# Folding the gate sums to 64 partitions before their product with ones

## The chip, the cores and the metric

The kernel runs on one NeuronCore of a Trainium2 chip. The metric is the device time of one execution in microseconds (us), the lower the better. Three timed executions of the kernel before took 1096.84, 1097.05 and 1098.40 us; the median is 1097.05 us. One more execution was recorded by the profiler, and all traces below are from it.

The engines are named as the profile does it: PE is the matrix engine (PEld its loading of stationary operands), DVE the vector engine, ACT the scalar engine, POOL the general engine (gpsimd), SP the one that issues the weight DMAs. Each engine works through its own list of instructions in order and waits at an instruction until what it needs is there.

## The reference, cut to what matters

```python
def reference(x, c, ada_w, ada_b, ...):              # x: 256 tokens x 1024, two layers
    c_act = jax.nn.silu(c)                            # c: 1 x 1024
    for l in range(DEPTH):
        mod = c_act @ ada_w[l] + ada_b[l]
        sh1, sc1, g1, sh2, sc2, g2, sh3, sc3, g3 = jnp.split(mod, N_ADA, axis=-1)
        n1 = modulate(rms_norm(h, norm_g[l, 0]), sh1, sc1)
        h = h + 0.5 * g1[:, None, :] * swiglu(n1, ...)
        n2 = modulate(rms_norm(h, norm_g[l, 1]), sh2, sc2)
        h = h + g2[:, None, :] * token_mixing(n2, ...)
        n3 = modulate(rms_norm(h, norm_g[l, 2]), sh3, sc3)
        h = h + 0.5 * g3[:, None, :] * swiglu(n3, ...)
    return rms_norm(h, final_g)
```

The change touches only how the gates g1, g2 and g3 (1024 numbers for each of the six sub-layers) are brought to all 128 partitions.

## The kernel before, in words

The two layers have three sub-layers each: a feed-forward network (FFN), the token mixer, and a second FFN. They run one after the other, with all 256 tokens at once. In the FFN, the 2816 hidden columns are cut into 11 slices (`idx` 0 to 10, `NS = 11`): for each slice a gate bank `g` and an up bank `u` are computed (`gate_up_mm`, then `gate_up_act`), and some slices later the down product `dn` (`down`). The mixer ends with eight gate products (`gate_mm`, tile `gt`), the output heads (`b_out`, `b_outT`, tiles `on`, `onf`, `odH`, `odL`), and then the branch products `yb` (`merge`) and `wo`.

All products are made in a split form: an operand in 32-bit floating point is taken as a high part (a rounded copy, made by ACT: `whi`, `hh`, `gh`) and a low part (what is left, made by DVE: `wlo`, `hl`, `gl`), and `mm3` (lines 85 to 88) forms a product as high·high, low·high and high·low. The weights come in by DMA into the ring `raw` (4 buffers), and `pump` splits them ahead of their use.

The gates are made in two steps. First `ada_gate` (line 276) multiplies a block of the weights with one element of silu(c) per partition and adds it to `gacc` (128 partitions x 1024 columns), eight times for each sub-layer; row 0 of `gacc` begins with the bias. What is then missing is the sum over the 128 partitions, and that sum on every partition. `gate_bcast` (lines 289 to 304) gives both by a product with a 128x128 matrix of ones: for each half of 512 columns, ACT makes `gh` (line 299), DVE makes `gl` (line 300), PE adds the products of ones with `gh` and with `gl` in one bank `gb` (lines 301, 302), and ACT writes half of the sum to `g` (tile `gbc`, line 304). `residual` uses it much later, at the end of the sub-layer.

`gate_bcast` is called once for each sub-layer: after slice 7 of each FFN (or when the weights of the next gate are about to be loaded, line 282), and in the mixer between the last gate product and the first `yb`. This document calls the six places A to F: A, FFN 1 of layer 0 (at 139.8 us of the trace); B, its mixer (323.2 us); C, its second FFN (451.3 us); D, FFN 1 of layer 1 (624.8 us); E, the second mixer (858.5 us); F, the last FFN (1028.5 us).

The order of instructions on each engine is not the order of the program text: a scheduler lays the instructions out at build time by its own costs and by what they depend on. POOL's list is short: it clears `gacc` (line 286), and raises small tiles to the power -1/2 (`pow_half`, line 124). `b2` tiles (tags `gh`, `gl`, `sg`, `on` and others) come from one ring of 8 buffers.

Of the kernel before, what the change touches and what calls it, by code (L numbers as in the profile page):

```python
# [13 lines left out]
F32 = mybir.dt.float32  # L14
F32R = mybir.dt.float32r
AF = mybir.ActivationFunctionType
ALU = mybir.AluOpType
AX = mybir.AxisListType

P = 128  # L20
# [22 lines left out]
def trunk(tc, a):  # L43
    nc = tc.nc
    with (
# [11 lines left out]
        def nm(s):  # L57
            uid[0] += 1
            return f"{s}_{uid[0]}"

        def gen(name="gen"):
            return ps.tile([P, 512], F32, tag="gen", bufs=4, name=nm(name))
# [4 lines left out]
        def b2(name, shape=(P, 512), dt=F32):  # L67
            return sb.tile(list(shape), dt, tag="b2", bufs=NB2, name=nm(name))
# [13 lines left out]
        def const(name, shape, dt=F32):  # L82
            return sb.tile(list(shape), dt, tag=name, bufs=1, name=name)
# [29 lines left out]
        onesr = const("onesr", [P, P], F32R)  # L113
        nc.scalar.copy(onesr, ones)
        for hf in range(2):
            x = slice(hf * 512, (hf + 1) * 512)
            bank = gen("cb")
# [162 lines left out]
        def gate_start(l, s):  # L280
            if owed:
                gate_bcast(*owed[0])
            owed.append((l, s))
            m = mod_of(l, s)
            m["gacc"] = sb.tile([P, D], F32, tag="gacc", bufs=1, name=nm("gacc"))
            nc.gpsimd.memset(m["gacc"], 0.0)
            nc.scalar.dma_start(m["gacc"][0:1, :], a["ada_b_row"][l, s:s + 1, :])

        def gate_bcast(l, s):
            m = mods[(l, s)]  # L290
            if (l, s) not in owed:
                return
            owed.remove((l, s))
            m["g"] = sb.tile([P, D], F32, tag="gbc", bufs=1, name=nm("gbc"))
            for hf in range(2):
                bank = gen("gb")
                x = m["gacc"][:, hf * 512:(hf + 1) * 512]
                gh, gl = b2("gh", dt=F32R), b2("gl", dt=F32R)
                nc.scalar.copy(gh, x)
                nc.vector.tensor_tensor(gl, x, gh.bitcast(F32), op=ALU.subtract)  # L300
                nc.tensor.matmul(bank, onesr, gh, start=True, stop=False, skip_group_check=True)
                nc.tensor.matmul(bank, onesr, gl, start=False, stop=True, skip_group_check=True)

                nc.scalar.mul(m["g"][:, hf * 512:(hf + 1) * 512], bank, 0.5)

# [255 lines left out]
        def ffn(i, nT, norm1, first, nT_next):  # L561
# [64 lines left out]
            for idx in range(start, NS):  # L626
                g, u = gen("g"), gen("u")
                gate_up_mm(g, u, unit(idx), nT)
                hT[idx] = gate_up_act(g, u)
                if idx == 7:  # L630
                    gate_bcast(l, s)
                if idx == 1:
                    hT[0] = first_T(hts)
                elif idx - 1 < NS - TAIL:
                    if idx == 2 and first is None:
                        down(0)
                    down(idx - 1)
                if idx == 4 and s == 0:
                    consts = mixer_loads(l)
                if idx == 7 and s == 0:  # L640
                    consts = mixer_consts(l, consts)
# [75 lines left out]
        def mixer(i, nT, norm1, consts, nT_next):  # L717
# [373 lines left out]
            b_outT(1)  # L1091
            gate_mm(7, 1)
            gate_bcast(l, 1)


# [310 lines left out]
```

## Time and profile before

| | |
|---|---|
| median of three runs | 1097.05 us (1096.84 to 1098.40) |
| the profiled execution | 1097.68 us |
| its span, first to last instruction | 1095.9 us |
| PE busy | 99% of the span, 7796 recorded products |
| DVE, ACT, POOL busy | 79%, 54%, 4% |
| granted PE clock, mean | 0.999 of full speed |

The profiled execution takes 1.8 us more than its span, which is start and end around the instructions. Products on PE overlap: one of 512 columns has a recorded duration of 0.39 us, but the next one begins 0.23 us after it. So what a product costs is read from the distance of two starts, not from its duration. On ACT and DVE too, an instruction begins about 0.1 us before the one ahead of it has ended, when nothing else holds it.

### The profile page before, as it was taken

How to read it: one execution, taken by the hardware profiler on the slowest of the kernel's cores; microseconds unless marked ns; L12 is line 12 of the kernel's file. 1: busy time of each engine (PE TensorE's matmuls, PEld its weight loads, DVE VectorE, ACT ScalarE, POOL GpSimd, SP SyncE). 2: the span in 40 equal slices, each digit the busy share in tenths (PEclk: the TensorE clock that was granted, in tenths of full speed). 3: DMA queues.
4: the chain of work that ended last, by engine and by line, in shares of the span. 5: the costliest groups of instructions: out<-in, count | busy, mean ns of one | idle time of the engine just before them, and what ended most of it. 6: DMA issues, size and time to landing. Idle time of an engine off the chain costs nothing.

```text
span 1095.9 us, 19235 instructions
## 1 busy us (share of the span) xinstructions
PE 1082.9 (99%) x7796; PEld 998.8 (91%) x7796; DVE 864.9 (79%) x1388; ACT 593.1 (54%) x916; POOL 44.5 (4%) x52
## 2 busy tenths in 40 slices
PE   8999999999999999999999999999999999999997
PEld 6989999898999899999989999989889998999996
DVE  5998986899978798886589886569988779766543
ACT  5564483558664554535455545435776547444432
POOL 1000000220010000000000000004000000000000
PEclk9999999999999999999999999999999999999999
DMA  8998996368745299997449987543865454876501
GB/s 315 380 368 336 380 335 219 120 263 332 264 172 193 86 376 357 347 377 266 150 152 357 365 288 285 202 165 126 297 236 189 157 190 183 315 267 229 197 19 39
DMA packets 44889, 271.12 MB, mean 247 GB/s; under 512 B 5880, under 2 KB 6648, under 8 KB 14848
## 3 DMA queue, kind: packets, MB, share of 16 engines
q1 hardware_dynamic: 42340, 267.93, 66.1%
q10 hardware_dynamic: 2460, 1.96, 0.6%
q8 instruction: 61, 1.00, 0.3%
q14 instruction: 28, 0.23, 0.1%
HBM read 268.82 MB, written 1.05 MB: 246 GB/s over the span
## 4 chain that ended last, share of the span: by engine, by line
PE 94%; DVE 3%; ACT 1%; issue 1%; POOL 0%; POOLq 0%
PE dn L87 6%; PE dn L88 6%; PE dn L86 6%; PE u L86 6%; PE g L86 6%; PE u L87 6%; PE g L88 6%; PE g L87 6%; PE u L88 6%; PE gt L86 3%; PE gt L88 3%; PE gt L87 3%; PE g L1199 2%; PE u L1199 2%; PE yb L88 1%; PE yb L87 1%
## 5 line engine op out<-in xcount | busy, mean ns | idle before, releaser
L330 DVE TENSOR_TENSOR wlo<-raw,whi 128x1024 fp32r<-128x1024 f32 x364 | 436.9, 1220 | 133.7 <-PE u L87 44.6
L328 ACT CAST whi<-raw 128x1024 fp32r<-128x1024 f32 x364 | 374.0, 1052 | 226.4 <-PE u L88 83.7
L86 PE MATMUL u<-nh,whi 128*128 128x256 f32 x592 | 164.0, 277 | 0.0
L86 PE MATMUL g<-nh,whi 128*128 128x256 f32 x592 | 164.0, 277 | 0.0
L87 PE MATMUL u<-nh,wlo 128*128 128x256 f32 x592 | 163.7, 277 | 0.0
L88 PE MATMUL g<-nl,whi 128*128 128x256 f32 x592 | 163.7, 277 | 0.0
L87 PE MATMUL g<-nh,wlo 128*128 128x256 f32 x592 | 163.7, 277 | 0.0
L88 PE MATMUL u<-nl,whi 128*128 128x256 f32 x592 | 163.6, 276 | 0.0
L86 PE MATMUL dn<-whi,hh 128*128 128x512 f32 (+1 forms) x326 | 126.0, 387 | 0.0
L87 PE MATMUL dn<-whi,hl 128*128 128x512 f32 (+1 forms) x326 | 125.9, 386 | 0.0
L88 PE MATMUL dn<-wlo,hh 128*128 128x512 f32 (+1 forms) x326 | 125.8, 386 | 0.0
L86 PEld LDWEIGHTS g<-nh,whi 128*128 128x128 f32 x592 | 111.2, 188 | 0.3
L87 PEld LDWEIGHTS g<-nh,wlo 128*128 128x128 f32 x592 | 111.2, 188 | 0.2
L86 PEld LDWEIGHTS u<-nh,whi 128*128 128x128 f32 x592 | 111.2, 188 | 0.1
L87 PEld LDWEIGHTS u<-nh,wlo 128*128 128x128 f32 x592 | 111.3, 188 | 0.0
L88 PEld LDWEIGHTS u<-nl,whi 128*128 128x128 f32 x592 | 111.2, 188 | 0.2
L88 PEld LDWEIGHTS g<-nl,whi 128*128 128x128 f32 x592 | 111.2, 188 | 0.0
L245 DVE CUSTOM_DVE_ANT_0 raw<-raw,cb 128x1024 f32<-128x1024 f32 x80 | 95.5, 1217 | 1.1 <-DMA raw<-in_ada_t_dram 0.9
L86 PE MATMUL gt<-nh,whi 128*128 128x256 f32 x256 | 73.7, 288 | 0.0
L88 PEld LDWEIGHTS dn<-wlo,hh 128*128 128x128 f32 x326 | 61.2, 188 | 12.4
L87 PEld LDWEIGHTS dn<-whi,hl 128*128 128x128 f32 x326 | 61.3, 188 | 11.1 <-DVE hl L546 0.2
L86 PEld LDWEIGHTS dn<-whi,hh 128*128 128x128 f32 x326 | 61.3, 188 | 11.1
(227 smaller groups left out, 2051.9 us busy)
## 6 DMA issues: line engine op xcount, KB each, us to landing
raw<-in_w_gu_dram SPq DMA_DIRECT2D x79, 1024.0 KB, 5.5
raw<-in_w_d_dram SPq DMA_DIRECT2D x41, 1024.0 KB, 6.4
raw<-in_ada_t_dram SPq DMA_DIRECT2D x40, 1024.0 KB, 6.8
raw<-in_ada_g_dram SPq DMA_DIRECT2D x24, 1024.0 KB, 6.3
raw<-in_w_in_dram SPq DMA_DIRECT2D x16, 1024.0 KB, 5.0
raw<-in_w_gate_dram SPq DMA_DIRECT2D x16, 1024.0 KB, 4.9
raw<-in_ada_t_dram SPq DMA_DIRECT2D x16, 512.0 KB, 6.5
raw<-in_w_gu_dram SPq DMA_DIRECT2D x32, 256.0 KB, 6.1
```

The lines of the kernel that those rows point to most:

```text
L86: nc.tensor.matmul(out, Lh, Rh, start=start, stop=False, skip_group_check=True)
L87: nc.tensor.matmul(out, Ll, Rh, start=False, stop=False, skip_group_check=True)
L88: nc.tensor.matmul(out, Lh, Rl, start=False, stop=stop, skip_group_check=True)
L245: queue("dve", nc.vector.tensor_tensor_reduce(r, r, cb, 1.0, 0.0, op0=ALU.mult, op1=ALU.add, accum_out=col[:, k:k + 1]))
L328: split[1] = nc.scalar.copy(hi, r)
L330: split[0] = nc.vector.tensor_tensor(lo, r, hi.bitcast(F32), op=ALU.subtract)
L1199: nc.tensor.matmul(bank[:, c * 256:(c + 1) * 256], W[:, w], N[:, k, :], start=x + y + k + c == 0, stop=y == 1 and k == NK - 1, skip_group_ ...
```

## The change

```diff
@@ gate_bcast: for each half hf, x = m["gacc"][:, hf * 512:(hf + 1) * 512]
-                gh, gl = b2("gh", dt=F32R), b2("gl", dt=F32R)
-                nc.scalar.copy(gh, x)
-                nc.vector.tensor_tensor(gl, x, gh.bitcast(F32), op=ALU.subtract)
-                nc.tensor.matmul(bank, onesr, gh, start=True, stop=False, skip_group_check=True)
-                nc.tensor.matmul(bank, onesr, gl, start=False, stop=True, skip_group_check=True)
+
+                gf = b2("gf", (64, 512))
+                nc.gpsimd.tensor_copy(gf, x[64:P, :])
+                nc.gpsimd.tensor_tensor(gf, gf, x[0:64, :], op=ALU.add)
+                gs = b2("gs", dt=F32R)
+                nc.scalar.copy(gs[0:64, :], gf)
+                nc.vector.tensor_tensor(gs[64:P, :], gf, gs[0:64, :].bitcast(F32), op=ALU.subtract)
+                nc.tensor.matmul(bank, onesr, gs, start=True, stop=True, skip_group_check=True)
 
                 nc.scalar.mul(m["g"][:, hf * 512:(hf + 1) * 512], bank, 0.5)
```

POOL adds the upper 64 partitions of `gacc` to the lower 64 (tile `gf`), ACT writes the high part of that to partitions 0 to 63 of `gs`, DVE the low part to partitions 64 to 127, and one product with ones sums all 128. Two b2 buffers are used for each half, as before. The scheduler then lays out the lists anew. Three places matter below.

ACT at place B, the end of the first mixer (the same at E). `whi` are weight splits, `odH` the high part of the heads' output, `gt` the activation of the last gate bank, `gbc` the result of the broadcast. Before:

```order
L328 CAST whi_3935<-raw_3701 128x1024
L299 CAST gh_3943<-gacc_2115 128x512
L299 CAST gh_3951<-gacc_2115 128x512
L980 CAST odH_3860<-onf_3907 128x4x128
L1003 ACTIVATE gt_3847<-gt_3866,bg_1184 128x256 x2
L304 ACTIVATE gbc_3941<-gb_3942 128x512
L304 ACTIVATE gbc_3941<-gb_3950 128x512
```

ACT's list at place B now:

```order
L331 CAST whi_3937<-raw_3703 128x1024
L983 CAST odH_3862<-onf_3909 128x4x128
L303 CAST gs_3948<-gf_3945 64x512
L1006 ACTIVATE gt_3849<-gt_3868,bg_1184 128x256 x2
L303 CAST gs_3957<-gf_3954 64x512
L307 ACTIVATE gbc_3943<-gb_3944 128x512
L331 CAST whi_3988<-raw_3703 128x1024
L307 ACTIVATE gbc_3943<-gb_3953 128x512
```

The two casts stood together ahead of `odH`; now the first stands behind `odH`, and the second behind `gt`.

DVE at the same place, before:

```order
L977 TENSOR_SCALAR onf_3907<-ont_3902,subg_1186 128x512
L300 TENSOR_TENSOR gl_3944<-gacc_2115,gh_3943 128x512
L300 TENSOR_TENSOR gl_3952<-gacc_2115,gh_3951 128x512
L981 TENSOR_TENSOR odL_3861<-onf_3907,odH_3860 128x4x128
L330 TENSOR_TENSOR wlo_3936<-raw_3701,whi_3935 128x1024
L330 TENSOR_TENSOR wlo_3985<-raw_3701,whi_3984 128x1024
```

DVE's list at place B now:

```order
L980 TENSOR_SCALAR onf_3909<-ont_3904,subg_1186 128x512
L984 TENSOR_TENSOR odL_3863<-onf_3909,odH_3862 128x4x128
L304 TENSOR_TENSOR gs_3948<-gf_3945,gs_3948 64x512
L333 TENSOR_TENSOR wlo_3938<-raw_3703,whi_3937 128x1024
L304 TENSOR_TENSOR gs_3957<-gf_3954,gs_3957 64x512
L333 TENSOR_TENSOR wlo_3989<-raw_3703,whi_3988 128x1024
```

The two low parts stood behind `onf` and ahead of `odL`; now they stand behind `odL`, with a weight split (`wlo`) between them. On PE the four `gb` products stood together between the last `gt` and the first `yb`; now two stand there.

DVE at place A, slice 7 of the first FFN (`sg` and `hl` belong to that slice; ISA rows are products of weights with c, each followed by the reading of its sum). Before:

```order
L543 TENSOR_TENSOR sg_1661<-u_1542,sg_1661 128x512
L300 TENSOR_TENSOR gl_1669<-gacc_766,gh_1668 128x512
L330 TENSOR_TENSOR wlo_1491<-raw_1394,whi_1490 128x1024
L546 TENSOR_TENSOR hl_1660<-sg_1661,hh_1659 128x512
L330 TENSOR_TENSOR wlo_1514<-raw_1394,whi_1513 128x1024
L245 ISA raw_1423,mraw_1046<-raw_1423,cb 128x1024
L245 ISA mraw_1046 128x1
L245 ISA raw_1423,mraw_1046<-raw_1423,cb 128x1024
L245 ISA mraw_1046 128x1
L300 TENSOR_TENSOR gl_1677<-gacc_766,gh_1676 128x512
L250 TENSOR_TENSOR msh_1049<-mraw_1046,abc 128x2
```

DVE's list at place A now:

```order
L546 TENSOR_TENSOR sg_1661<-u_1542,sg_1661 128x512
L333 TENSOR_TENSOR wlo_1491<-raw_1394,whi_1490 128x1024
L549 TENSOR_TENSOR hl_1660<-sg_1661,hh_1659 128x512
L333 TENSOR_TENSOR wlo_1514<-raw_1394,whi_1513 128x1024
L245 ISA raw_1423,mraw_1046<-raw_1423,cb 128x1024
L245 ISA mraw_1046 128x1
L245 ISA raw_1423,mraw_1046<-raw_1423,cb 128x1024
L245 ISA mraw_1046 128x1
L304 TENSOR_TENSOR gs_1671<-gf_1668,gs_1671 64x512
L250 TENSOR_TENSOR msh_1049<-mraw_1046,abc 128x2
L304 TENSOR_TENSOR gs_1680<-gf_1677,gs_1680 64x512
```

The first low part moved back behind the ISA rows, next to the second. PE at place A, where before only the last of the four products stood (the others stood among the `dn` products ahead of this piece):

```order
L86 MATMUL g_1740<-nh_119,whi_1425 128x256
L87 MATMUL g_1740<-nh_119,wlo_1426 128x256
L88 MATMUL g_1740<-nl_120,whi_1425 128x256
L86 MATMUL u_1741<-nh_119,whi_1425 128x256
L302 MATMUL gb_1675<-gl_1677,onesr 128x512
L87 MATMUL u_1741<-nh_119,wlo_1426 128x256
L88 MATMUL u_1741<-nl_120,whi_1425 128x256
```

PE's list at place A now, from the end of the `dn` block on:

```order
L583 MATMUL dn_851<-wlo_1391,hh_1494 128x264
L583 MATMUL dn_851<-wlo_1391,hh_1494 128x248
L305 MATMUL gb_1667<-gs_1671,onesr 128x512
L86 MATMUL dn_848<-whi_1537,hh_1659 128x512
L305 MATMUL gb_1676<-gs_1680,onesr 128x512
L86 MATMUL g_1742<-nh_119,whi_1425 128x256
L87 MATMUL g_1742<-nh_119,wlo_1426 128x256
```

Both products now stand after the `dn` block and ahead of slice 8's first `g`; before, ten products of slice 8 stood ahead of the last `gb`. One `dn` of the next slice has come in between the two.

## Rows read from the trace of the kernel before

**Rows 1.** The page: shares of the chain that ended last, by engine.

```profile
PE 94%; DVE 3%; ACT 1%; issue 1%; POOL 0%; POOLq 0%
```

**Rows 2.** Tile gb, its first product: duration min/median/max in ns, first and last start.

```profile
L301 PE MATMUL gb<-gh,onesr x12: 392/399/497, 139.8 to 1030.4; 128*128 128x512 f32 x12
```

**Rows 3.** Timeline of PE, place C: start us, us, engine, line, operation, out<-in, shapes.

```profile
451.30 0.40 PE L301 MATMUL gb<-gh,onesr 128*128 128x512 f32 x1
```

**Rows 4.** Timeline of DVE, place C.

```profile
446.36 0.69 DVE L300 TENSOR_TENSOR gl<-gacc,gh 128x512 fp32r<-128x512 f32 x1
```

**Rows 5.** Timeline of PE, place D.

```profile
624.82 0.40 PE L301 MATMUL gb<-gh,onesr 128*128 128x512 f32 x1
```

**Rows 6.** Timeline of DVE, place D.

```profile
612.71 1.28 DVE L300 TENSOR_TENSOR gl<-gacc,gh 128x512 fp32r<-128x512 f32 x2
```

**Rows 7.** Timeline of PE, place B.

```profile
323.15 0.40 PE L301 MATMUL gb<-gh,onesr 128*128 128x512 f32 x1
...
324.10 0.28 PE L86 MATMUL yb<-oaH,whi 128*128 128x256 f32 x1
```

**Rows 8.** Timeline of ACT, place B; in brackets idle time ahead and its releaser.

```profile
320.17 1.05 ACT L328 CAST whi<-raw 128x1024 fp32r<-128x1024 f32 x1 [0.34 <-PE gt L88]
...
322.17 0.62 ACT L980 CAST odH<-onf 128x512 fp32r<-128x512 f32 x1
323.35 0.84 ACT L1003 ACTIVATE gt<-gt,bg 128x256 f32<-128x256 f32 x2 [0.56 <-PE gt L88]
```

**Rows 9.** Timeline of DVE, place B.

```profile
321.26 0.75 DVE L977 TENSOR_SCALAR onf<-ont,subg 128x512 f32<-128x512 f32 x1
...
323.13 0.68 DVE L981 TENSOR_TENSOR odL<-onf,odH 128x512 fp32r<-128x512 f32 x1
323.73 1.22 DVE L330 TENSOR_TENSOR wlo<-raw,whi 128x1024 fp32r<-128x1024 f32 x1
```

**Rows 10.** Timeline of DVE, the last sum into gacc ahead of place B.

```profile
241.08 1.27 DVE L276 SCALAR_TENSOR_TENSOR gacc<-raw,ccol,gacc 128x1024 f32<-128x1024 f32 x1
```

**Rows 11.** Timeline of POOL from 86 to 324 us.

```profile
216.64 3.43 POOL L814 TENSOR_SCALAR qsc<-hr 128x8 f32<-128x8 f32 x1
...
227.50 0.92 POOL L814 TENSOR_SCALAR qsc<-hr 128x8 f32<-128x8 f32 x1
...
315.94 1.01 POOL L124 TENSOR_TENSOR or<-oms,mhalf 128x4 f32<-128x4 f32 x1 [3.70 <-DVE oms L959]
323.27 0.96 POOL L286 MEMSET gacc<- 128x1024 f32 x1 [6.32 <-DVE gl L300]
```

**Rows 12.** Timeline of ACT, place A.

```profile
139.09 0.61 ACT L299 CAST gh<-gacc 128x512 fp32r<-128x512 f32 x1
```

**Rows 13.** Timeline of DVE, place A.

```profile
139.22 0.69 DVE L543 TENSOR_TENSOR sg<-u,sg 128x512 f32<-128x512 f32 x1 [0.93 <-ACT sg L542]
...
145.85 0.69 DVE L300 TENSOR_TENSOR gl<-gacc,gh 128x512 fp32r<-128x512 f32 x1
146.45 0.15 DVE L250 TENSOR_TENSOR msh<-mraw,abc 128x2 f32<-128x2 f32 x1
```

**Rows 14.** Timeline of PE, place A.

```profile
145.15 0.28 PE L86 MATMUL g<-nh,whi 128*128 128x256 f32 x1
...
146.19 0.28 PE L86 MATMUL u<-nh,whi 128*128 128x256 f32 x1
146.59 0.50 PE L302 MATMUL gb<-gl,onesr 128*128 128x512 f32 x1
146.93 0.28 PE L87 MATMUL u<-nh,wlo 128*128 128x256 f32 x1
```

**Rows 15.** Timeline of DVE, place F.

```profile
1028.72 0.68 DVE L543 TENSOR_TENSOR sg<-u,sg 128x512 f32<-128x512 f32 x1
```

**Rows 16.** Timeline of PE, place F.

```profile
1027.44 0.39 PE L86 MATMUL dn<-whi,hh 128*128 128x512 f32 x1
...
1032.25 0.39 PE L87 MATMUL dn<-whi,hl 128*128 128x512 f32 x1
```

## The prediction

> **What bounds the kernel now.** The first view is the chain that ended last, by engine: PE has 94% of it [rows 1]. So a product that goes is worth its pitch on PE, a wait that PE gets is paid in full unless PE later waits for something else, and work on DVE, ACT or POOL costs only what PE waits for it. The second view is the tile gb: 12 halves, each with a product of gh and one of gl [rows 2]; the change removes 12 of the 24. The third is the timeline of PE at the six broadcasts, beside those of DVE and ACT. The reader should see there how far ahead of PE the low parts are written. At C the second gl begins at 446.36 and takes 0.69, so it ends 4.25 us before PE comes to its first gb at 451.30 [rows 3, 4]; at D the pair ends at 612.71 + 1.28 = 613.99, 10.8 us before 624.82 [rows 5, 6]. At A, B, E and F there is next to no lead: at A PE comes to the last gb after a product at 146.19 and issues it at 146.59, 0.05 after its gl has ended at 145.85 + 0.69 = 146.54 [rows 13, 14]. At B the four products pass without a wait, 324.10 - 323.15 = 0.95, or 0.24 each [rows 7].
>
> **What is removed.** 12 products at 0.24 make -2.9 us if nothing else moved. ACT's cast and DVE's subtraction stay, one each per half; I cost them at 0.61 and 0.68 as now [rows 9, 12], since columns stay 512 and only partitions are halved. No row shows an operation of this kind on 64 partitions, so the other end is half of it; that is a rival below.
>
> **What is added on POOL.** A copy and an add for each half, in series, ahead of the cast. gacc is complete long before it is needed: ahead of B its last sum ends at 241.08 + 1.27 = 242.35 [rows 10]. POOL's list holds the fold at B and E behind the second `or`, which ends at 315.94 + 1.01 = 316.95 [rows 11]; nothing else waits on POOL before gacc is cleared. What one of the two takes, no row shows. The low end is half of the clearing of 1024 columns, 0.96 / 2 = 0.48 us; the high end is the longest row of a POOL instruction here, 3.43 us [rows 11]. I take values near the first, since it is the only row of many columns: 0.5 for the copy, 1.0 for the add that reads two tiles, some 1.6 per half with a short gap. Both halves are folded by about 320.2. In the new order the first cast comes at 322.56 and the second at 324.09 (below), so the fold is hidden as long as a half takes under (324.09 - 316.95) / 2 = 3.6 us; at the high end the last would end at 316.95 + 4 x 3.43 = 330.7, 6.6 us too late, and cost that at B and E each, up to 1113. At A, C, D and F POOL has nothing to do in between and far more time. That POOL slows DVE by reading beside it is not shown either way; from 317 to 320 it would stretch some five DVE instructions, and I leave 0.3 us for it in the range.
>
> **B and E, where the order costs most.** The scheduler put the casts later on ACT and the low parts later on DVE. By the rows of now: onf ends at 321.26 + 0.75 = 322.01 [rows 9]. ACT is free since 320.17 + 1.05 = 321.22 and waits for it; odH (0.62) ends at 322.66 [rows 8]. The first cast of gs, 0.1 overlapped, ends at 323.17. DVE makes odL (0.68) from 322.69 to 323.37, and the first low part to 323.97. PE, which came to it at 323.15, issues the first gb at 324.02. On ACT gt is still released by PE's last gt product, at 323.35, and ends at 324.19 [rows 8]; only then comes the second cast, 324.09 to 324.70. On DVE wlo (1.22 [rows 9]) stands between and runs from 323.89 to 325.11, so the second low part is made from 325.03 to 325.71. PE issues the second gb at 325.76 and the first yb at 326.00, where it now begins at 324.10 [rows 7]: +1.9 us. Behind the waiting gb stand all the yb products, which need nothing from it. The casts and low parts behind on ACT and DVE wait for yb's results too, so nothing catches up. E repeats B's lists: +1.9 again.
>
> **A.** Now the sg multiplication ends at 139.91 [rows 13] and gl follows it on DVE; without that gl and with ACT's cast of whi taking gh's place at 139.09 [rows 12], the following wlo begins 0.5 us earlier (140.17 in place of 140.68 by 1.05 + 0.03 after 139.09), and so does everything down to the first low part, 145.35 to 146.03. A small msh follows, then the second, 146.01 to 146.70. PE, freed of three products and 0.2 of waits, comes to the first gb 0.9 earlier than it now comes to slice 8's first g (145.15 [rows 14]), at 144.3, and waits to 146.08. Then come the moved dn (0.23) and the second gb at 146.75, and g begins at 146.99: +1.84. What now still lies ahead of it in time and then no more: the last gb with its wait, 146.93 - 146.19 less one product of 0.115, or 0.63 [rows 14], and the dn, 0.23. Left: +1.0 us.
>
> **C, D, F.** At C and D the lead of 4 and 10 us covers a shift of 1 us, and two products of four go: -0.48 each. At F PE needs now from the first to the 17th dn 1032.25 - 1027.44 = 4.81 [rows 16], with four gb among them. Then: 12 dn at 0.23 reach the first gb at 1030.20; its low part follows sg (ended at 1029.40 [rows 15]) at once and is ready at 1030.0. The second, behind hl, is ready at 1031.36; PE comes at 1031.35, issues at 1031.41, and the 17th dn at 1031.65: -0.6.
>
> **The sum.** A +1.0, B +1.9, E +1.9, C -0.5, D -0.5, F -0.6: +3.2 us. The profiled execution took 1097.68, so 1100.9 by it; it lies 0.6 above the median of the runs shown, 1097.05, and against that I predict 1100.3.
>
> **A rule on POOL.** The two qsc instructions of one mixer, equal in shape, take 3.43 and then 0.92 [rows 11]: the first of a kind can take 2.5 us longer. [...]
>
> **The rivals.** (1) The fold is late on POOL: the first copy and first add at B and E take 3.43 each and the second pair 0.7 each. Then the first half is ready at 323.8, the first cast ends at 324.4, gt follows to 325.2, the second cast ends at 325.9, wlo holds DVE to 326.3, and yb begins at 327.2 in place of 326.0: +1.2 at each, 1102.7. For it speak the two qsc rows; against it, that `or`, also first after a long pause, takes 1.01. (2) Work on 64 partitions takes half the time. Then at B the low parts end at 323.63 and 325.03 and yb begins at 325.32: +1.2 in place of 1.9; A +0.4, F -0.7, C and D as before: +1.2, 1098.3, no change that can be told. Against it: nothing in the rows ties a duration to partitions; they go with columns (0.61 for 512, 1.05 for 1024 [rows 8, 12]). (3) Not slower but faster: at B and E the second gs is there when PE comes. It decides at 323.39, when PE would have the first gb behind it; the second low part would have to be ready 2.3 us sooner than I have it. Then B and E give -0.5 each and, with A +1.0, C, D and F, the sum is -1.6, 1095.5; with A's three gb and waits saved as well it is -3.4, 1093.6. Against it: the second cast stands behind gt, which PE itself releases at 323.35 [rows 8].
>
> **How the numbers follow.** Forecast 0.62 (own range 1099.3 to 1101.4: 0.3 for each of A, B, E), rival 1 0.14, rival 2 0.16, rival 3 0.08. A measurement of this kernel tells 0.2%, 2.2 us, from no change: faster is below 1094.9, slower above 1099.2. Rival 2 and the forecast's lower edge are "same", 0.18; the forecast and rival 1 make slower 0.74; faster 0.08. The range leaves out rival 3 and the costlier half of rival 1: 1098.1 to 1102.8.
>
> **What would show it.** Right: PE idle of about 0.9 and 1.5 us ahead of the two gb at B and E, released by DVE's gs; 1.8 us ahead of the first gb at A; none at C and D. Gf on POOL done by 321 at B. Wrong: POOL as the releaser of ACT's cast of gs (rival 1); gs rows near 0.3 us (rival 2); no idle ahead of gb (rival 3). If the idle is there and the time is not longer, the step that failed is that PE does not catch up behind it.

## The result, and the profile after

The changed kernel takes 1106.36 us (median of 4 runs, 1105.47 to 1107.35), the kernel before 1097.07 beside it: a ratio of 1.0082, with an interval of 1.0070 to 1.0094. It is slower, by three times the 3.2 us of the sum. The profiled execution is the fastest of the four, 1105.47, with a span of 1103.7 against 1095.9; the mean granted clock of the four is 0.994 to 0.996, against 0.999 in the profiled execution before.

First the view of PE's waits, by what was waited for (us in total, times, longest). It has one row with gb that has no counterpart before:

```profile
PE gb L305 <- DVE gs L304: 6.8, 5, 1.9
```

The timeline of PE shows two of these at B [rows 7]; the last `gt` product, the two `gb` and the first `yb`:

```profile
324.84 0.28 PE L88 MATMUL gt<-nl,whi 128*128 128x256 f32 x1
325.98 0.50 PE L305 MATMUL gb<-gs,onesr 128*128 128x512 f32 x1 [0.86 <-DVE gs L304]
328.04 0.47 PE L305 MATMUL gb<-gs,onesr 128*128 128x512 f32 x1 [1.57 <-DVE gs L304]
328.35 0.28 PE L86 MATMUL yb<-oaH,whi 128*128 128x256 f32 x1
```

DVE at the same place [rows 9]:

```profile
323.07 0.75 DVE L980 TENSOR_SCALAR onf<-ont,subg 128x512 f32<-128x512 f32 x1
324.51 0.69 DVE L984 TENSOR_TENSOR odL<-onf,odH 128x512 fp32r<-128x512 f32 x1 [0.69 <-ACT odH L983]
325.23 0.69 DVE L304 TENSOR_TENSOR gs<-gf,gs 64x512 fp32r<-64x512 f32 x1
325.95 1.23 DVE L333 TENSOR_TENSOR wlo<-raw,whi 128x1024 fp32r<-128x1024 f32 x1
327.21 0.69 DVE L304 TENSOR_TENSOR gs<-gf,gs 64x512 fp32r<-64x512 f32 x1
```

and ACT [rows 8]:

```profile
324.38 0.61 ACT L303 CAST gs<-gf 64x512 fp32r<-64x512 f32 x1
325.16 0.84 ACT L1006 ACTIVATE gt<-gt,bg 128x256 f32<-128x256 f32 x2 [0.16 <-PE gt L88]
325.89 0.61 ACT L303 CAST gs<-gf 64x512 fp32r<-64x512 f32 x1
```

The waits stand where they were foreseen, 0.86 and 1.57 for "about 0.9 and 1.5", and DVE's row is the releaser. E has the same two, 0.85 and 1.56. The low part takes 0.69 on half the partitions, as on all. POOL [rows 11] had long made the first half and had the second at 321.97 + 2.33 = 324.30, ahead of its cast at 325.89:

```profile
318.82 0.61 POOL L300 COPY gf<-gacc 64x512 f32<-64x512 f32 x1
319.50 1.29 POOL L301 TENSOR_TENSOR gf<-gf,gacc 64x512 f32<-64x512 f32 x1
320.86 1.03 POOL L300 COPY gf<-gacc 64x512 f32<-64x512 f32 x1
321.97 2.33 POOL L301 TENSOR_TENSOR gf<-gf,gacc 64x512 f32<-64x512 f32 x1
```

At A, PE's timeline has the foreseen wait too, but look at the time from one row to the next behind it [rows 14]:

```profile
145.36 0.53 PE L305 MATMUL gb<-gs,onesr 128*128 128x512 f32 x1 [1.92 <-DVE gs L304]
145.69 0.63 PE L86 MATMUL dn<-whi,hh 128*128 128x512 f32 x1
146.27 0.76 PE L305 MATMUL gb<-gs,onesr 128*128 128x512 f32 x1
146.83 0.41 PE L86 MATMUL g<-nh,whi 128*128 128x256 f32 x1
147.05 0.41 PE L87 MATMUL g<-nh,wlo 128*128 128x256 f32 x1
```

Two `g` products stand 0.22 apart where they stood 0.115 apart. The view of busy time by stretch says why. Its columns are the stretch, its length, busy us and instructions of PE, PEld, DVE, ACT and POOL, then the clock granted to PE, the DMA share and GB/s. After the change, behind A's wait, at B's waits, behind them, and around E's:

```profile
143.00:145.40 2.40, 0.48 (x4) 0.27 (x3) 2.34 (x6) 0.00 (x0) 0.00 (x0) 1.00 0.84 321
145.40:148.60 3.20, 3.20 (x12) 2.49 (x13) 3.14 (x5) 2.67 (x4) 0.00 (x0) 0.54 0.98 364
148.60:152.00 3.40, 3.40 (x30) 3.40 (x30) 2.16 (x4) 3.37 (x5) 0.00 (x0) 0.93 0.75 258
325.00:328.30 3.30, 0.87 (x4) 0.48 (x3) 2.80 (x4) 2.87 (x5) 0.32 (x1) 1.00 0.68 283
328.30:332.00 3.70, 3.70 (x32) 3.65 (x32) 0.63 (x1) 1.18 (x2) 0.00 (x0) 1.00 0.01 1
860.00:864.80 4.80, 2.38 (x17) 1.90 (x17) 3.67 (x5) 4.01 (x7) 1.82 (x2) 1.00 0.60 218
864.80:869.00 4.20, 4.20 (x24) 4.16 (x24) 0.00 (x0) 0.60 (x1) 0.00 (x0) 0.62 0.02 5
869.00:872.00 3.00, 3.00 (x26) 3.00 (x25) 2.29 (x3) 1.06 (x1) 0.00 (x0) 0.96 0.17 25
```

The kernel before has 1.00 in the same stretches:

```profile
145.40:148.60 3.20, 3.08 (x26) 2.84 (x25) 2.83 (x7) 1.47 (x3) 0.95 (x1) 1.00 0.94 387
859.50:865.00 5.50, 5.50 (x48) 5.50 (x47) 3.02 (x4) 3.01 (x5) 0.08 (x1) 1.00 0.36 115
```

Behind the waits at A and at E the granted clock is 0.50 of full speed for 3.4 us each, from 145.6 to 149.0 and from 865.9 to 869.3 (read in stretches of 0.1 us). A stretch of 3.2 us at 0.54 does 1.5 us less work, and 3.4 us at 0.93 another 0.2; at E 4.2 us at 0.62 and 3.0 at 0.96 make 1.6 and 0.1. So 1.7 us were lost at each, on top of the wait. Behind B, with the same lists and nearly the same waits as E, the clock stayed at 1.00.

Each remaining product of PE can be set beside the same product before, and the difference followed through the span. It is -1.2 from the first stages on (kernels with and without the change show this start or not, from one execution to the next); A adds 3.0, B 2.4, C -0.5, D -0.7, E 3.8, F nothing; the other 0.9 is small waits such as one of 0.6 at 930 us (`u` released by ACT's `sg`), not looked into. That makes the 7.8 of the two spans; the 9.3 between the medians has no trace of its own. Of the 7.8, 3.4 are the clock; without it A costs 1.3, B 2.4 and E 2.1.

### The profile page after: what moved, and what is told of

Its sections match the earlier page's. It is cut to its first block, busy times and chain, and to the rows that moved or that the text cites. A ratio compares the mean times of both kernels' runs of the same rounds, so it can differ in the third digit from the quotient of the medians.

```text
span 1103.7 us, 19259 instructions
## 1 busy us (share of the span) xinstructions
PE 1082.5 (98%) x7784; PEld 997.0 (90%) x7784; DVE 873.2 (79%) x1388; ACT 594.3 (54%) x916; POOL 86.9 (8%) x76
## 4 chain that ended last, share of the span: by engine, by line
PE 88%; DVE 6%; DMA 2%; issue 2%; ACT 1%; POOL 0%; POOLq 0%; SPq 0%; ACTq 0%; DVEq 0%
PE dn L87 6%; PE dn L88 6%; PE dn L86 6%; PE u L86 6%; PE u L87 6%; PE g L87 6%; PE g L88 6%; PE g L86 6%; PE u L88 6%; PE gt L86 3%; PE gt L87 3%; PE gt L88 2%; DMA raw<-in_w_gu_dram 2%; DVE wlo L333 2%; PE yb L88 1%
## 5 line engine op out<-in xcount | busy, mean ns | idle before, releaser
L545 ACT ACTIVATE sg<-g 128x512 f32<-128x512 f32 x41 | 24.4, 598 | 88.2 <-PE g L88 88.1
```

Source lines behind the costliest of these rows:

```text
L545: nc.scalar.activation(sg, g, AF.Silu)
```

## The experiments

All but two were timed in several rounds beside the kernel before, whose median was 1097.70, 1097.52 and 1097.36 in the three groups (e1 to e4, e5 to e8, e9 to e11).

**e1_early: the same products, their parts written earlier.**

Fold, casts and low parts of both halves become a function of their own, `gate_prep`; `gate_bcast` keeps the products and `gbc`:

```diff
+                if idx == 6:
+                    gate_prep(l, s)
                 if idx == 7:
                     gate_bcast(l, s)
...
+            gate_prep(l, 1)
             b_out(1)
```

At F its fold leaves out the last two sums into `gacc`.

> The changed kernel with its fold, casts and low parts written earlier in the program (FFN: after slice 6; mixer: before the second heads' output), the products left where they are. Theory 1 (the cost is the order: PE waits for low parts that the lists put too late, and its clock falls after the wait): no idle ahead of any gb product, no stretch of half clock at A or E, and the twelve products saved at 0.24 us show: 1093.3 to 1095.0 us. Theory 2 (the cost is POOL: its fold is slow or slows DVE): all 24 POOL instructions are still there, so the time stays above 1101 us.

1098.31 us, ratio 1.0007 (0.9998 to 1.0015). Nothing waits for gb, the clock behind A, B and E is 1.00, and 8 us of the loss are gone. The gain of 12 products doesn't show. The low parts in the mixers now stand ahead of the head norms (`on`) on DVE, and PE waits 1.0 there in each mixer. From its view of PE's waits:

```profile
PE ont L986 <- DVE on L983: 2.0, 2, 1.0
PE wt L953 <- DVE xb L947: 1.0, 1, 1.0
```

The chain behind the first row begins on POOL, whose list now has the second add of the fold behind `or`. ACT's second cast waits 3.30 for that add, and DVE's low part 2.81 for the cast (ACT in the first mixer; the second is alike):

```profile
314.66 0.62 ACT L300 CAST gs<-gf 64x512 fp32r<-64x512 f32 x1 [3.30 <-POOL gf L298]
```

The wait at `wt` (304 us) has no low part just ahead of it and was not looked into. Theory 2 with its 1101 is out, though in this order a fold that POOL's list puts late has a share in what is left. Theory 1's number was missed by 3 us, in part for these waits of the experiment's own.

**e2_late: the kernel before, with only the mixers' casts and low parts at the places where the change puts them.** `follow` puts an instruction behind another on its engine:

```diff
+                    follow(ch, late["odH"] if hf == 0 else late["gt"])
+                    follow(cl, late["odL"] if hf == 0 else late["wlo"])
```

> The kernel before, without any fold and with its two products, but with the casts and low parts of the two mixers held to the places that the changed kernel's lists give them (first cast behind odH, second behind gt; first low part behind odL, second behind wlo). Theory 1: PE idles ahead of gb at B and E by about 2 us each, and after it the clock may fall for some 3 us: 1100.5 to 1104.5 us. Theory 2: nothing is folded and POOL is as before, so 1096.5 to 1097.7 us.

1100.75 us, ratio 1.0026 (1.0016 to 1.0035), inside theory 1's range. No fold, no `gs`, four products as before, and 3 us more: the order alone does it, by 1.4 at each mixer in the difference of the products. The waits are not the 2 us expected but 0.5 at each place; from the last `gt` to the first `yb` it is 2.05 where it was 1.07, and the last gb now follows behind five `yb`. The clock in the stretches behind B and E is 1.00. Its waits for gb:

```profile
PE gb L307 <- DVE gl L301: 0.6, 2, 0.3
...
PE gb L306 <- ACT gh L300: 0.4, 2, 0.2
```

**e3_idlefold: the kernel before, with POOL folding into a tile that nobody reads.**

```diff
+                nc.gpsimd.tensor_copy(gf, x[64:P, :])
+                nc.gpsimd.tensor_tensor(gf, gf, x[0:64, :], op=ALU.add)
                 gh, gl = b2("gh", dt=F32R), b2("gl", dt=F32R)
```

> The kernel before, with POOL folding gacc at the same six places into a tile that nobody reads (24 more POOL instructions, none of them waited for by the products). Theory 1: 1096.3 to 1097.8 us, no difference. Theory 2: slower by the POOL part of the loss, 1100 us or more.

1099.04 us, ratio 1.0017 (1.0008 to 1.0026): 1.3 more, where theory 1 had none and theory 2 more. The difference of the PE products grows at one place, by 1.6 at 252 us, where `pt` waits for the softmax (`p`). There POOL folds beside DVE. DVE's timeline before:

```profile
245.94 1.22 DVE L245 CUSTOM_DVE_ANT_0 raw<-raw,cb 128x1024 f32<-128x1024 f32 x1
```

and in e3, beside POOL's add of 246.91 to 248.21:

```profile
246.98 2.32 DVE L245 CUSTOM_DVE_ANT_0 raw<-raw,cb 128x1024 f32<-128x1024 f32 x1
```

DVE's instruction began 0.07 after POOL's add and took 1.10 longer than before. In the changed kernel POOL's list holds this fold to 318.8 us, past that place, and the stretched DVE rows (at 416 to 425 us, ahead of C) have no waiting PE behind them. So this price belongs to e3's place of the fold; the pair e5 and e6 below shows none beyond its noise in another place. Two of e3's eleven runs took 1101.85 and 1102.70, with a mean clock of 0.996 where the others have 0.998 or 0.999: that fits low clock there too, in a kernel where nothing waits for gb, but neither has a trace.

**e4_fill: the changed kernel with 4 and 7 products of ones by ones on PE, ahead of the two gb of each mixer.**

```diff
+                if s == 1:
+                    for _ in range((4, 7)[hf]):
+                        pe = nc.tensor.matmul(bank.rearrange("p (r x) -> p r x", r=4), onesr, ones4, start=True, stop=True,
+                                              skip_group_check=True)
```

> The changed kernel, with 4 products of ones with ones ahead of the first gb and 7 ahead of the second in each mixer, into the same bank, which the real product then overwrites: PE is busy while it waits, ACT, DVE and POOL have the same lists. If the clock falls because PE idled: granted clock 1.00 right after the gb products at B and E, the 1.5 us that E lost to the clock come back, less 0.1 to 0.3 us by which the fillers outlast the wait: 1103.8 to 1105.3 us beside 1106.4. If the clock falls for another reason or by chance: half clock again in about half of such places, 1105.5 to 1107.3 us.

1104.39 us, ratio 1.0060 (1.0048 to 1.0073). Behind E the clock is 1.00; behind A, which has no fillers, it fell again (0.71, then 0.77):

```profile
145.40:148.60 3.20, 2.48 (x9) 2.01 (x10) 3.11 (x6) 2.19 (x4) 0.00 (x0) 0.71 0.70 248
865.00:869.00 4.00, 4.00 (x24) 3.36 (x24) 1.91 (x2) 2.71 (x5) 0.00 (x0) 1.00 0.36 146
```

By the medians 2.0 us came back, though gs is as late as ever: at B the second one begins 4.13 behind the start of `onf`, and 4.14 in the changed kernel. The profiled execution is the slowest of the five, 1105.89, and loses about 1.5 at 280 us, where no gb stands.

**e10_fill_all: e4 with fillers at A as well.**

```diff
-                if s == 1:
-                    for _ in range((4, 7)[hf]):
+                if s == 1 or (l, s) == (0, 0):
+                    for _ in range((4, 7)[hf] if s else (8, 2)[hf]):
```

> e4_fill with the same filler at A too: 8 products of ones by ones ahead of the first product of ones and 2 ahead of the second. The results are late as before, PE only has work while it waits. Theory 1 (the clock falls because PE has stood still): no stretch of low clock behind A, B or E, mean clock as before (0.998 to 0.999), and about 1.5 us less than e4_fill's 1104.4: 1102.4 to 1103.6. Rival (the clock falls for another reason, such as the run of 512-column products itself): the low stretches stay, 1104 or more.

1102.72 us (1101.61 to 1103.64), ratio 1.0044 (1.0030 to 1.0058), clock 0.998 to 0.999 in all five runs. The view by stretch, behind A, B and E:

```profile
145.40:148.60 3.20, 2.60 (x14) 1.81 (x13) 3.07 (x6) 1.71 (x3) 0.00 (x0) 1.00 0.84 328
...
328.30:332.00 3.70, 3.70 (x30) 3.60 (x30) 0.30 (x2) 0.99 (x3) 0.00 (x0) 1.00 0.00 0
...
864.80:869.00 4.20, 4.20 (x33) 3.85 (x32) 0.79 (x2) 1.49 (x3) 0.00 (x0) 1.00 0.01 4
```

32 products that compute nothing of use make the changed kernel 3.6 us faster (1106.36 - 1102.72, from two groups whose kernels before lie 0.3 apart the other way). What they change is that PE has work while it waits for gs. That is the part of the loss that is the clock, less the time by which fillers outlast a wait.

**e9_ffnearly: e1's edit in the FFNs but the last alone; mixers as in the changed kernel.**

```diff
+                if idx == 6 and (l, s) != (1, 2):
+                    gate_prep(l, s)
```

> The changed kernel with fold, casts and low parts of the FFNs (but the last) written one slice earlier; the mixers are as in the changed kernel. Theory 1 (places are independent, and at A the wait and the half clock behind it cost 2.9 us where the products alone give 0.7 back): A turns from a loss into a gain of 0.5 to 1.0 and the mixers keep theirs, so 3.4 to 4.0 us below the changed kernel's 1106.4: 1102.4 to 1103.0. Rival (what A lost is only shifted to the next wait): 1105 or more.

1102.03 us, ratio 1.0041 (1.0028 to 1.0055). That is 0.4 below theory 1's range, and the rival is out. A's wait is gone, and the difference behind A is -1.0. Its profile shows the clock low behind B as well as E, in the stretches 325 to 328 and 865 to 869:

```profile
325.00:328.00 3.00, 2.42 (x10) 2.36 (x11) 0.43 (x1) 1.17 (x2) 0.00 (x0) 0.55 0.01 1
...
865.00:869.00 4.00, 4.00 (x24) 4.00 (x23) 0.21 (x1) 0.23 (x2) 0.00 (x0) 0.62 0.02 5
```

Its five runs took 1099.5, 1101.85, 1102.03, 1102.4 and 1104.1 us, at a mean clock of 0.999, 0.997, 0.997, 0.996 and 0.996. The program and its lists are the same each time. The slowest is the profiled one, with two stretches of low clock worth 1.7 each; the mean clocks of the others fit one stretch or two, and none in the fastest. The rest of the spread is not the clock: the first stages alone differ by 1.2 from one execution to the next.

**e7_nolow: the kernel before without the low parts and their 12 products.**

```diff
-                nc.vector.tensor_tensor(gl, x, gh.bitcast(F32), op=ALU.subtract)
-                nc.tensor.matmul(bank, onesr, gh, start=True, stop=False, skip_group_check=True)
-                nc.tensor.matmul(bank, onesr, gl, start=False, stop=True, skip_group_check=True)
+                nc.tensor.matmul(bank, onesr, gh, start=True, stop=True, skip_group_check=True)
```

> The kernel before in its own order without the low parts and their 12 products (the low part of the gate sums is left out of the result): what 12 products fewer are worth when no wait is added. By the pitch of these products in the trace of before 12 times 0.2275 is 2.7 us less: 1094.6 to 1095.4 beside 1097.7. If the products were hidden beside something else, 1096.5 to 1097.7.

1094.86 us, ratio 0.9967 (0.9955 to 0.9979): 2.7 less, as 12 times 0.2275 said. DVE's 12 subtractions go with the products here. The saving that the change aims at is real, and the changed kernel loses it to its waits and to the clock behind them.

**e5_moved and e6_moved2p: the change, and the kernel before, in an order in which nothing waits.** In both, the mixers' products come after the second merge step, and in the FFNs but the last casts and low parts come one slice earlier:

```diff
             gate_mm(7, 1)
-            gate_bcast(l, 1)
+            gate_prep(l, 1)
...
             merge(1)
+            gate_bcast(l, 1)
...
+                if idx == 6 and (l, s) != (1, 2):
+                    gate_prep(l, s)
```

> The changed kernel with its steps spread: in the mixers the fold, casts and low parts stay where the changed kernel has them, and the two products of ones come after the second merge step; in the FFNs (but the last) fold, casts and low parts are written one slice earlier and the products stay; the last FFN is as in the changed kernel. Theory 1 (the loss is the waits ahead of the products and the clock that falls behind them): no product of ones waits, no stretch at half clock, and the time is 2.7 us (12 products of 0.2275) below the kernel with the same order and two products, less up to 1.3 us that the fold on POOL cost when nobody read it: 1094.5 to 1096.5. Theory 2 (fold, casts and low parts cost by being there): no gain against two products in this order, 1097.5 or more.

> The kernel before (two products, no fold) with its casts, low parts and products in the order of e5_moved, so that order and change can be told apart. Both theories: order alone moves little, since the products of the kernel before waited for little: 1096.7 to 1098.5.

e5 takes 1094.32 us (1094.22 to 1095.01), ratio 0.9967 (0.9956 to 0.9979); e6 1096.72, ratio 0.9988 (0.9979 to 0.9996). In this order the change is worth 2.4 us, and PE's waits in e5 have no row with gb. Against the 2.7 of the products that leaves 0.3 for the fold and all else that it adds, which is less than either interval is wide (1.9 to 2.5 us). The lists of the two are not alike throughout: e6 has its low parts ahead of `odL` on DVE, e5 behind. The clock is 0.998 to 0.999. e5 is the version that beats both kernels: 12 us below the changed kernel, with the same instructions.

**e8_samepart and e11_swap: why the low parts stand apart.** In the changed kernel DVE's rows around a low part begin 0.72 apart, with 0.03 idle on either side, where rows of the same 0.69 overlapped by 0.09 before [rows 4]; and PE comes 0.14 behind its end, not 0.05 (0.06 at the first gb of B and E). Is it that they read partitions 0 to 63 and write 64 to 127?

In e8 the fold is made on all 128 partitions, and the low part reads and writes 64 to 127:

```diff
-                nc.vector.tensor_tensor(gs[64:P, :], gf, gs[0:64, :].bitcast(F32), op=ALU.subtract)
+                nc.vector.tensor_tensor(gs[64:P, :], gf[64:P, :], gs[64:P, :].bitcast(F32), op=ALU.subtract)
```

In e11 the two parts change places:

```diff
-                nc.vector.tensor_tensor(gs[64:P, :], gf, gs[0:64, :].bitcast(F32), op=ALU.subtract)
+                nc.vector.tensor_tensor(gs[0:64, :], gf, gs[64:P, :].bitcast(F32), op=ALU.subtract)
```

> The changed kernel with the fold on all 128 partitions (POOL copies both halves across and adds 128 partitions), so that the low part reads and writes the same 64 partitions. If the longer pitch of the low parts in the changed kernel (0.72 us with 0.03 idle on either side, beside 0.60 of the full-height low part before) and the longer way to the product (0.14 beside 0.05) come from reading partitions 0 to 63 and writing 64 to 127, the low parts overlap their neighbours again and start 0.60 apart. If they come from the height of 64 partitions, they stay at 0.69 and apart. Its time says little, since POOL has more to do: 1105 to 1110 by theory 1.

> The changed kernel with the high part on partitions 64 to 127 and the low part on 0 to 63. If the low parts of the changed kernel stand 0.03 apart from their neighbours on DVE and 0.14 ahead of their product because they write from partition 64 up, they now overlap (0.60 apart, 0.05 ahead). If the height of 64 partitions does it, nothing changes. Time as the changed kernel: 1105 to 1107.5.

One execution each, 1107.56 and 1106.26 us. In both every low part still takes 0.69 and stands apart from the row ahead, by 0.03 in e8 and by 0.03 to 0.1 in e11. DVE at C in e11:

```profile
450.40 0.15 DVE L253 TENSOR_TENSOR sc<-mraw,abc 128x2 f32<-128x2 f32 x1
450.58 0.69 DVE L304 TENSOR_TENSOR gs<-gf,gs 64x512 fp32r<-64x512 f32 x1
451.31 0.16 DVE L254 SCALAR_TENSOR_TENSOR ma<-sc,ngc 128x2 f32<-128x2 f32 x1
```

Neither the shift alone nor the upper half as target is the cause. Nor is the height alone: at D of the changed kernel DVE makes both low parts in a row, and the two take 1.29 together, so they overlap by 0.08 as full-height rows do:

```profile
616.92 1.29 DVE L304 TENSOR_TENSOR gs<-gf,gs 64x512 fp32r<-64x512 f32 x2
```

What stands apart is a low part and a neighbour of another kind. In all three kernels the low part has an operand that starts at partition 64 (its output, all of its operands, or one input), and its neighbours start at 0; in e11, where one input starts at 0 and one at 64, even the two at D stand 0.1 apart. That points to the first partition and not to the height, but no run varied it alone, so the cause stays open. In e8's profile the clock fell behind B (0.64) and E (0.53) and not behind A.

## Why the prediction was wrong

- **The step that failed** is in its first paragraph: "a wait that PE gets is paid in full". It was paid in more than full. In the profiled execution PE stood still for 1.92 us at A and for 2.41 in all at E, and behind each the granted clock was 0.50 for 3.4 us; behind B, after 2.43 in all, it was 1.00. The sum had no term for it and the rivals none either. Measured: 1.7 us at A and 1.7 at E in the profiled execution; 3.6 on the medians, by e10_fill_all. Shown by e4 and e10: with work in the wait the clock was back (1.00 behind E in e4, behind A and E in e10), with gs as late. e9's runs agree: of one kernel, the execution with the highest mean clock is the fastest by 2.4 us. Why it fell behind B in one execution (0.55 in e9's) and not in another stays open here. The medians differ by 9.3, 6.1 more than the sum; about 3.6 of that is the clock, 1.4 the terms below, and some 1 us of it was not traced.
- **B and E** were rightly placed and undersized, 2.4 and 2.1 for 1.9. From the end of `onf` to the first `yb` I had 326.00 - 322.01 = 3.99 us; it took 328.35 - 323.82 = 4.53. Three steps on DVE (odL to gs, gs to wlo, wlo to gs) took 0.12 each more, since the low part stands 0.03 from its neighbours where 0.09 of overlap was reckoned; PE came 0.14 behind the last one instead of 0.05; and from a gb that waited to the next product it is 0.31, not 0.24. Rows of before had the 0.05 and the overlap, but for 128 partitions. That the term of 128 would hold for 64 was a choice: the duration came out right (0.69), the overlap did not.
- **A** had +1.0 and cost 1.3 without the clock. The wait was foreseen at 1.8 and is 1.92.
- **C and D** gave 0.5 and 0.7 for 0.5 each: no wait there, as foreseen.
- **F** was to give 0.6 and gave nothing. Its low parts have next to no lead, ending at 1037.68 and 1039.11, and with 0.14 from there to the product both gb come 0.1 to 0.2 late; its rows [rows 16]:

```profile
1038.82 0.40 PE L86 MATMUL dn<-whi,hh 128*128 128x512 f32 x1
1039.26 0.47 PE L305 MATMUL gb<-gs,onesr 128*128 128x512 f32 x1
1039.57 0.40 PE L87 MATMUL dn<-whi,hl 128*128 128x512 f32 x1
```

  0.44 and 0.31 stand where 0.23 each was reckoned.
- **Rival 1** (POOL late) is out: a copy takes 0.61 to 1.61 and an add 1.27 to 2.33 (one copy, beside seven instructions of DVE, 8.26), and no cast of the mixers waits for them. The estimate of 0.5 and 1.0 was near the low end, and "done by 321 at B" was missed: it was 324.30, which cost nothing there. The reading of the `qsc` rows as the first of a kind was wrong. In the kernel before, the second mixer has the same 3.43 again, and both times two-input instructions of DVE run beside it and end 0.1 before it (POOL, then DVE):

```profile
752.24 3.43 POOL L814 TENSOR_SCALAR qsc<-hr 128x8 f32<-128x8 f32 x1
752.61 0.68 DVE L810 TENSOR_TENSOR qr<-q,q 128x512 f32<-128x512 f32 x1
753.21 2.35 DVE L330 TENSOR_TENSOR wlo<-raw,whi 128x1024 fp32r<-128x1024 f32 x2
```

  So these rows are more likely POOL held up by DVE, as in the last section. Nor was the first copy of the fold a slow one: at 87.69 us, it starts 0.17 after the last sum into `gacc` has ended and takes 0.61.
- **Rival 2** (half the partitions, half the time) is out by the rows of 0.61 and 0.69. **Rival 3** (no waits) holds only once the order is changed: e5, 1094.3 where it had 1093.6 to 1095.5.
- **The range** of the forecast itself, 1099.3 to 1101.4, is not quite what its margins give (0.3 at each of three places and 0.3 for POOL make 1099.4 to 1101.5); nothing hangs on it.
- The direction was right, and for the reason given, the order of the instructions on ACT and DVE: e2_late shows that this order alone costs 3 us with nothing folded.

## What to carry to other kernels

Halving the products of a step is worth their pitch only if their input is there; read from the new lists of ACT and DVE when it will be, and move the product to where it is no longer waited for, since its result was not needed soon (B's is first read at 362.65, 34 us later). The wait of 1.92 us at A cost another 1.7 behind it: look at the granted clock of the stretch behind a wait before calling it cheap, and where a wait can't be avoided, products of no use ahead of it can pay, as the 3.6 us of e10 show. Price work put on POOL by what DVE loses beside it (1.10 us in one instruction of e3).

## What was not expected of the hardware

Side by side, POOL and DVE took longer in several places. Of DVE's 1024-wide instructions with two inputs, 1.22 us each elsewhere, one took 1.62 (at 578.18 us) and one 2.31 (at 422.47) beside the fold; POOL's copy, 0.61 at 87.69, took 8.26 at 570 us, beside seven such DVE instructions in a row:

```profile
570.46 8.26 POOL L300 COPY gf<-gacc 64x512 f32<-64x512 f32 x1 [8.98 <-DVE nl L432]
```

In e3 POOL's add ends 1.23 after the DVE instruction of 2.32 has begun, which then runs for another 1.09, near the 1.22 of a whole one. So it looks as if DVE waited there for POOL's add; why was not shown. On PE it cost 1.6 us in e3; in e5 nothing that stands out of the noise.
